# Low parts of later weights in the second scan instead of the first, three small operations on ScalarE, and transposes at the front of a unit

## The chip, the core and the metric

One Trainium2 chip, one of its cores. A core has TensorE (PE, matmuls and transposes; PEld is its weight load), VectorE (DVE), ScalarE (ACT), GpSimd (POOL) and SyncE (SP, which issues DMAs); DMAs are also issued on POOL's queue. Each engine works through its own instructions in the order in which they were written into the program. The metric is the device time of one execution in microseconds (us), the median of three.

## The reference

A hybrid layer for 512 tokens and 16 learned meta tokens, width 1024, all fp32. Two token mixers run on the same normalised input, and a channel mixer of experts follows them. What the change touches is the second token mixer (SSD, like Mamba-2), and the preparation of two weights of the expert part:

```python
xbc = jax.nn.silu(causal_dwconv(xbc, conv_w, conv_b))     # 4 taps
xs, Bm, Cm = split_cols(xbc, (SSD_D_INNER, SSD_BC, SSD_BC))

def ssd_chunk_step(S, inp):                               # chunks of 64 tokens
    xdt, a, Bc, Cc = inp
    acum = jnp.cumsum(a, axis=1)
    seg = jnp.exp(-jnp.abs(acum[:, :, None] - acum[:, None, :]))
    cb = jnp.einsum('btgn,bsgn->btsg', Cc, Bc)
    y = jnp.einsum('btsgr,btsg,bsgrp->btgrp', seg, cb, xdt)
    y = y + jnp.einsum('btgn,bgrpn,btgr->btgrp', Cc, S, jnp.exp(acum))
    to_end = jnp.exp(acum[:, -1:] - acum)
    S = S * jnp.exp(acum[:, -1])[..., None, None] + jnp.einsum('bsgn,bsgr,bsgrp->bgrpn', Bc, to_end, xdt)
    return S, y

y = y.reshape(Bsz, L, SSD_D_INNER) * jax.nn.silu(z)
y = rmsnorm(y.reshape(Bsz, L, SSD_GROUPS, SSD_D_INNER // SSD_GROUPS), ...)
```

The first mixer (GLA) is a chunked scan of the same kind with gates. In the expert part the weight w_q (here wpq, 16 blocks) and the table of down projections for a dense share of the experts (puT, 16 blocks) are multiplied with the normalised tokens.

## The kernel before, in words

Matmuls keep fp32 accuracy with three products of split operands: each operand is a high part (hi, rounded by ACT to the fast matmul type) and a low part (lo = raw − hi, by DVE). `unit` loads a weight block of 128x1024 on SP's queue (`raw`, three buffers), makes `whi` on ACT and `wlo` on DVE. For the 32 blocks of wpq and puT, which come late in the program, `unit_c` reads the low part back from DRAM (`lo_d`). Somebody has to make it earlier: that is `lows`, a generator with 64 steps, one for each half block of 128x512. A step loads `zr`, ACT copies it to `zh`, DVE subtracts in place (`zh<-zr,zh`) and a DMA on POOL's queue writes `lo_d<-zh`. The loads are on POOL's queue too (L148). `zh` has 2 buffers and `zr` 3, so ACT can begin a `zh` only when the `lo_d` write two steps before has landed. What is written is read first in the expert part, at about 814 us, some 120 us behind the last stage that the change touches.

The program ahead of the expert part has these stages. From about 80 to 302 us runs the first scan (`gproj`, `gscan`: projections q, k, v and the gate g, with tiles `vt`, `go`, `kn`, `ed`, and the chunk loop), with all 64 steps of `lows` merged into it. From 302 to 345 us come the rest of `sproj(0)` and the second scan's first decays. From 345 to 690 us the second scan runs: `sscan(g)` for four groups g of 8 heads, four chunk pairs of 128 tokens each, and beside it `sproj(g + 1)`, or, beside group 3, the gates of the merge.

`sproj(g)` has six convolution units (BT, CT, and four of xT) and then the projection z. A unit `conv` is 48 matmuls of 128x264 into `pa` and `pb`, two copies `rw` on ACT, the first tap on DVE (L287, which also adds the bias), three more taps on DVE (L289), and a silu (tanh on ACT, `silu_t`, and a DVE operation at L279). `turn(b)` transposes the xT of two units earlier (XLAG = 2) on PE into `px` (L310) and `pxm` (L313), and ACT copies them to `xs` and `xsm`.

`sscan(g)` does for each chunk pair: `ssp` (state contributions, L358), the DVE addition into `sS`, `py` (L425, 16 small matmuls with `xs`), `pi` (L429, L430, with the state `sS`), DVE operations on `y`, a square with sum on ACT, `ry` on DVE and POOL, the normalisation (L392, DVE), the transpose `pyt`, and, for the next chunk pair, `decays`: `pr` (L383, L384), a subtraction on DVE, the absolute value (L387, DVE: it masks the sign bit) and the exponential on ACT. `px`, `pxm`, `ssp`, `py`, `pi`, `pyt` and `pr` all take their PSUM tile from one ring of 4 buffers.

`drive((n, generator), ...)` merges generators by shares: each gets its turn in proportion to its n. Out of the order so written a scheduler sets each engine's instruction order, and the pools' buffer counts add waits.

## Time and profile before

| | us |
|---|---|
| three runs | 2184.10, 2188.85, 2195.99 |
| median | 2188.85 |
| the profiled execution | 2189.25 |
| its span | 2187.5 |
| PE busy in the span | 2083.8 (95%) |
| DVE busy | 1584.0 (72%) |
| ACT busy | 884.0 (40%) |
| POOL busy | 607.6 (28%) |

A span is cut into stages by their first matmuls; for each stage a view of the profile gives the busy time of each engine, the granted clock of PE and the share of the DMA engines. Another lists, for one engine and a stretch, what it waited for: the instruction that waited, the engine and instruction that released it, the sum, the count and the longest. A third lists single instructions in order of time with the idle time before each, and a fourth groups instructions by line and shape, with the mean duration of one.

### The profile page before, as it was taken

What the parts mean: (1) busy time and instruction counts of PE and PEld (TensorE: products, weight loads), DVE (VectorE), ACT (ScalarE), POOL (GpSimd) and SP (SyncE); (2) the same over time, 40 slices, a digit from 0 to 9 for tenths busy, and PEclk for the clock granted to TensorE, in tenths of its full rate; (3) what the DMA queues carried; (4) which work ended last, traced back from release to release, by engine and by line L of the source; (5) the groups of instructions that cost most, each with busy time, mean ns of one, the idle gap of its engine ahead of it and who ended that gap; (6) DMA issues with size and microseconds to landing.
All of it is one profiled execution on the core that took longest, in us unless ns stands there. A gap on an engine that the chain in (4) does not pass through costs nothing. (4 is left out here: it accounts for less than half of the span.)

```text
span 2187.5 us, 33055 instructions
## 1 busy us (share of the span) xinstructions
PE 2083.8 (95%) x12458; PEld 1825.2 (83%) x12458; DVE 1584.0 (72%) x2751; ACT 884.0 (40%) x1414; POOL 607.6 (28%) x564
## 2 busy tenths in 40 slices
PE   7988899999999998999999898999999999999997
PEld 6766778777777988989999887898998998898996
DVE  5374667787854668889899678877677777777775
ACT  5544433333333454455455432333333333333332
POOL 0253423343540000000000133343443333343331
PEclk9999999999999999999999999999999999999999
DMA  4557532212235877778667899989888888888883
GB/s 155 176 198 237 202 102 71 75 64 83 68 106 178 265 249 244 238 265 304 221 225 270 314 315 321 335 279 320 290 304 280 293 304 300 305 282 312 289 290 144
DMA packets 198432, 507.17 MB, mean 232 GB/s; under 512 B 16720, under 2 KB 89040, under 8 KB 196608
## 3 DMA queue, kind: packets, MB, share of 16 engines
q1 hardware_dynamic: 149440, 312.10, 42.2%
q0 software_dynamic: 48832, 192.96, 24.9%
q8 instruction: 97, 1.59, 0.3%
q14 instruction: 63, 0.52, 0.1%
HBM read 448.38 MB, written 56.62 MB: 231 GB/s over the span
## 5 line engine op out<-in xcount | busy, mean ns | idle before, releaser
L80 ACT ACTIVATE whi<-raw 128x1024 fp32r<-128x1024 f32 x433 | 458.5, 1059 | 517.4 <-PE pA L87 275.0
L83 DVE TENSOR_TENSOR wlo<-raw,whi 128x1024 fp32r<-128x1024 f32 x385 | 481.7, 1253 | 139.4 <-ACT whi L80 135.7
L86 PE MATMUL pA<-hh,whi 128*128 128x384 f32 x1024 | 346.3, 338 | 0.2 <-ACT ga L913 0.2
L88 PE MATMUL pA<-hh,wlo 128*128 128x384 f32 x1024 | 345.7, 338 | 0.5 <-DMA wlo<-lo_d 0.5
L87 PE MATMUL pA<-hl,whi 128*128 128x384 f32 x1024 | 345.9, 338 | 0.0
L989 POOL DMA_INDIRECT u<-in_pu,ix x128 | 176.4, 1378 | 298.9 <-ACT gh L1037 207.6
L989 POOL DMA_INDIRECT u<-in_pv,ix x128 | 170.9, 1335 | 281.0 <-ACT gh L1037 236.8
L1003 DVE SCALAR_TENSOR_TENSOR hacc<-u,acg,hacc 128x1024 f32<-128x1024 f32 x128 | 164.5, 1285 | 115.3 <-DMA u<-in_pv,ix 114.6
L1050 PE MATMUL va<-wlo,gh 128*128 128x512 f32 x768 | 239.9, 394 | 7.9 <-DVE wlo L83 7.9
L1050 PE MATMUL va<-whi,gh 128*128 128x512 f32 x768 | 239.7, 394 | 4.9 <-ACT whi L80 4.9
L997 DVE SCALAR_TENSOR_TENSOR scr<-u,hg 128x1024 f32<-128x1024 f32 x128 | 156.5, 1223 | 99.6 <-DMA u<-in_pu,ix 99.3
L87 PEld LDWEIGHTS pA<-hl,whi 128*128 128x128 f32 x1024 | 192.6, 188 | 4.2
L86 PEld LDWEIGHTS pA<-hh,whi 128*128 128x128 f32 x1024 | 192.1, 188 | 4.0 <-ACT ga L913 0.3
L1037 ACT ACTIVATE gh<-ga 128x384 fp32r<-128x384 f32 x128 | 67.2, 526 | 314.6 <-PE va L1050 293.7
L88 PEld LDWEIGHTS pA<-hh,wlo 128*128 128x128 f32 x1024 | 192.1, 188 | 0.7 <-DMA wlo<-lo_d 0.7
L1050 PEld LDWEIGHTS va<-wlo,gh 128*128 128x128 f32 x768 | 145.6, 190 | 40.6 <-DVE wlo L83 9.8
L1050 PEld LDWEIGHTS va<-whi,gh 128*128 128x128 f32 x768 | 144.4, 190 | 28.4 <-ACT whi L80 5.3
L86 PE MATMUL pk<-whi,hh 128*128 128x512 f32 x256 | 104.3, 407 | 6.7 <-ACT vt L80 6.3
L88 PE MATMUL pya<-oyh,wlo 128*128 128x256 f32 x384 | 108.5, 282 | 1.6 <-DVE wlo L83 1.6
L86 PE MATMUL pya<-oyh,whi 128*128 128x256 f32 x384 | 107.3, 280 | 0.0
L87 PE MATMUL pya<-oyl,whi 128*128 128x256 f32 x384 | 107.2, 279 | 0.0
L88 PE MATMUL pk<-whi,hl 128*128 128x512 f32 x256 | 102.3, 399 | 0.0
(910 smaller groups left out, 4473.9 us busy)
## 6 DMA issues: line engine op xcount, KB each, us to landing
raw<-in_puT SPq DMA_DIRECT2D x128, 512.0 KB
raw<-in_pv SPq DMA_DIRECT2D x128, 512.0 KB
raw<-in_wup SPq DMA_DIRECT2D x48, 512.0 KB
wlo<-lo_d SPq DMA_DIRECT2D x48, 512.0 KB
W_d<-stg POOLq DMA_DIRECT2D x12, 2048.0 KB
wb<-W_d SPq DMA_DIRECT2D x32, 768.0 KB
lo_d<-zh POOLq DMA_DIRECT2D x64, 256.0 KB
raw<-in_wpq SPq DMA_DIRECT2D x32, 512.0 KB
```

The source lines that it names most:

```text
L80: S.activation(out=o, in_=i, func=f, **kw)
L83: eng.tensor_tensor(o, x, y, op=op)
L86: T.matmul(o, lh, rh, start=first, stop=False)
L87: T.matmul(o, lh, rl, start=False, stop=False)
L88: T.matmul(o, ll, rh, start=False, stop=last)
L989: g_ = G.indirect_dma_start(out=u, out_offset=None, in_=a[tab], in_offset=bass.IndirectOffsetOnAxis(ap=ix[:, i, k:k + 1], axis=0))
L997: V.scalar_tensor_tensor(scr, u, 1.0, hg[:, i], op0=OP.mult, op1=OP.mult, accum_out=ac_[:, k:k + 1])
L1003: V.scalar_tensor_tensor(hacc[:, i], u, ac_[:, k:k + 1], hacc[:, i], op0=OP.mult, op1=OP.add)
L1037: i = S.activation(out=gh, in_=ga, func=AF.Copy)
L1050: T.matmul(va[t][c], x[:, cs], y[:, 512 * c:512 * c + 512], start=st_, stop=en_)
```

## The change

Four edits. The 64 steps of `lows` leave the first scan: they are merged with the end of `sproj(0)` (4 by the table), with the groups of the second scan (16 each) and the gates; `zh` gets 3 buffers and `zr` 4, in the pool `sg` of the second scan, and `zr` is loaded on SP's queue. The writes to `lo_d` stay on POOL's queue. The first tap, the absolute value and the normalisation become ACT activations (Identity with scale and bias, Abs, Copy with scale). And in a step of `sproj`, `turn` stands ahead of `conv` (or z) instead of behind it. The matmuls are the same in number and shape.

```diff
                 if 0 < n <= len(srcs):
-                    his[n - 1] = pool.tile([128, 512], F32R, name="zh", bufs=2)
+                    his[n - 1] = pool.tile([128, 512], F32R, name="zh", bufs=3)
                     act(his[n - 1], raws[n - 1], AF.Copy)
                 if n < len(srcs):
-                    raws[n] = pool.tile([128, 512], F32, name="zr", bufs=3)
-                    G.dma_start(raws[n], srcs[n])
+                    raws[n] = pool.tile([128, 512], F32, name="zr", bufs=4)
+                    nc.sync.dma_start(raws[n], srcs[n])
                 yield
...
                 cv = sp.tile([128, L], F32, name="cv")
-                V.tensor_scalar(cv, rw[:, 0:L], convw[:, b, 0:1], convb[:, b:b + 1], op0=OP.mult, op1=OP.add)
+                act(cv, rw[:, 0:L], AF.Identity, scale=convw[:, b, 0:1], bias=convb[:, b:b + 1])
...
                 for b in range(4 + XLAG):
+                    if b >= XLAG:
+                        turn(b - XLAG, x_[b - XLAG])
                     if b < 4:
                         x_.append(sp.tile([128, L], F32, name="xT", bufs=XLAG + 1))
                         conv(4 * g + b, x_[b])
                     else:
                         next(z_)
-                    if b >= XLAG:
-                        turn(b - XLAG, x_[b - XLAG])
                     yield
...
-                    V.tensor_scalar(sgm.bitcast(I32), sgm.bitcast(I32), 0x7FFFFFFF, None, op0=OP.bitwise_and)
+                    act(sgm, sgm, AF.Abs)
                     act(sgm, sgm, AF.Exp, scale=-1.0)
...
                 def norm(y, ry):
-                    V.tensor_scalar(y, y, ry, None, op0=OP.mult)
+                    act(y, y, AF.Copy, scale=ry)
...
-                lz = mix2.enter_context(tc.tile_pool(name="lz", bufs=1))
-                lw = lows(lz)
                 g1 = gproj(1)
-                drive((8, gscan(0)), (4, take(g1, 4)), (14, take(lw, 14)))
-                drive((8, g1), (32, take(lw, 32)))
+                drive((8, gscan(0)), (4, take(g1, 4)))
+                drive((8, g1))
                 p0 = sproj(0)
-                drive((8, gscan(1)), (6, take(p0, 6)), (20, lw))
+                drive((8, gscan(1)), (6, take(p0, 6)))
...
-            drive((4, p0))
+            lw = lows(sg)
+            drive((4, p0), (4, take(lw, 4)))
             for g in range(3):
-                drive((9, sscan(g)), (10, sproj(g + 1)))
-            drive((9, sscan(3)), (16 - NGT, gates(0, 16 - NGT, sg, 2)))
+                drive((9, sscan(g)), (10, sproj(g + 1)), (16, take(lw, 16)))
+            drive((9, sscan(3)), (16 - NGT, gates(0, 16 - NGT, sg, 2)), (16, lw))
```

What the scheduler makes of it is seen in the built order of each engine. The writes to `lo_d` show where the 64 steps come to stand: 16 ahead of group 0 (between the scans), 31 in group 0, 17 in group 1, none in groups 2 and 3.

On ACT, in the first scan, at the second projection of v (`vt` copies it out of PSUM; − is before, + after; the numbers behind pk count PSUM tiles):

```order
-L80 ACTIVATE zh<-zr 128x512 x2
-L80 ACTIVATE vt<-pk_1413 128x512
-L80 ACTIVATE vt<-pk_1414 128x512
-L80 ACTIVATE vt<-pk_1415 128x512
-L80 ACTIVATE zh<-zr 128x512
-L80 ACTIVATE vt<-pk_1416 128x512
+L80 ACTIVATE whi<-raw 128x1024 x3
+L80 ACTIVATE vt<-pk_1314 128x512
+L80 ACTIVATE vt<-pk_1315 128x512
+L80 ACTIVATE vt<-pk_1316 128x512
+L80 ACTIVATE vt<-pk_1317 128x512
 L80 ACTIVATE vm<-pke 16x512
```

The copies `zh` are gone from between the copies `vt`; only weights' high parts and `vt` are left.

On DVE, in group 0 of the second scan, the second half of a chunk pair, before (from the silu of one xT unit to that of the next):

```order
L279 SCALAR_TENSOR_TENSOR xT<-silu_t,cv 128x528
L83 TENSOR_TENSOR y<-y,xd 128x512
L387 TENSOR_SCALAR sgm<-sgm 128x512
L83 TENSOR_TENSOR y<-y,zt 128x512
L283 MEMSET rw 128x3
L83 TENSOR_TENSOR sgm<-sgm,cb 128x512
L83 TENSOR_TENSOR wlo<-raw,whi 128x1024
L176 TENSOR_SCALAR ry<-sy 128x1
L287 TENSOR_SCALAR cv<-rw,c_cst_96 128x528
L392 TENSOR_SCALAR y<-y,ry 128x512
L289 SCALAR_TENSOR_TENSOR cv<-rw,c_cst_96,cv 128x528 x3
L283 MEMSET rw 128x3
```

and the same place after:

```order
L83 TENSOR_TENSOR zh<-zr,zh 128x512
L83 TENSOR_TENSOR y<-y,zt 128x512
L83 TENSOR_TENSOR sgm<-sgm,cb 128x512
L83 TENSOR_TENSOR wlo<-raw,whi 128x1024
L176 TENSOR_SCALAR ry<-sy 128x1
L83 TENSOR_TENSOR zh<-zr,zh 128x512 x2
L289 SCALAR_TENSOR_TENSOR cv<-rw,c_cst_96,cv 128x528 x2
L83 TENSOR_TENSOR zh<-zr,zh 128x512
L289 SCALAR_TENSOR_TENSOR cv<-rw,c_cst_96,cv 128x528
L83 TENSOR_TENSOR zh<-zr,zh 128x512
L283 MEMSET rw 128x3
L279 SCALAR_TENSOR_TENSOR xT<-silu_t,cv 128x528
```

The tap of L287, the mask of L387 and the norm of L392 are gone, and five subtractions of lows stand in the stretch, two of them where the norm stood behind `ry`. At the start of a chunk pair `sS<-sS,ssp` now stands ahead of `wlo`, where it stood behind it.

On PE, in group 0, around the transposes `px`, `pxm` (L310, L313) and the chunk pair's `ssp` and `py`, before:

```order
L253 MATMUL pa<-hh,wlo 128x264
L253 MATMUL pb<-hh,wlo 128x264
L310 MATMUL px<-c_cst_79,xT 128x128 x4
L313 MATMUL pxm<-c_cst_79,xT 16x128
L358 MATMUL ssp<-xw,bt 128x512 x2
L425 MATMUL py<-xs,sgm 64x64 x16
L429 MATMUL pi<-sS,CT 64x512
```

and the same transposes after:

```order
L253 MATMUL pa<-hh,wlo 128x264
L253 MATMUL pb<-hh,wlo 128x264
L310 MATMUL px<-c_cst_79,xT 128x128 x4
L313 MATMUL pxm<-c_cst_79,xT 16x128
L250 MATMUL pa<-hh,whi 128x264
L251 MATMUL pa<-hl,whi 128x264
L250 MATMUL pb<-hh,whi 128x264
```

Behind the transposes comes now a whole convolution unit of 48 matmuls, and only then `ssp` and `py`, where before these two followed at once.

## Rows read from the trace of the kernel before

**Rows 1.** The page, part 1: busy us, share of the span, instructions.

```profile
PE 2083.8 (95%) x12458; PEld 1825.2 (83%) x12458; DVE 1584.0 (72%) x2751; ACT 884.0 (40%) x1414; POOL 607.6 (28%) x564
```

**Rows 2.** Stages: stretch, length, busy us (count) by engine, PE clock, DMA share, GB/s.

```profile
80.00:302.00 222.00, 194.39 (x1035) 155.13 (x1034) 131.81 (x186) 96.33 (x183) 96.06 (x147) 0.94 0.63 209
302.00:345.00 43.00, 42.22 (x240) 34.52 (x240) 23.73 (x36) 14.39 (x33) 11.70 (x10) 1.00 0.23 77
345.00:434.00 89.00, 82.90 (x614) 67.34 (x612) 70.53 (x95) 31.35 (x61) 36.00 (x31) 0.98 0.21 69
```

**Rows 3.** Waits of PE, 80 to 302: total us, times, longest us.

```profile
PE pkd L635 <- DVE ed L83: 8.7, 4, 4.0
PE pk L86 <- ACT vt L80: 6.3, 4, 3.7
PE pa L250 <- DVE go L279: 4.3, 1, 4.3
...
PE pb L250 <- DVE go L279: 2.3, 1, 2.3
```

**Rows 4.** Waits of ACT, 80 to 302, same columns.

```profile
ACT zh L80 <- DMA lo_d<-zh: 62.9, 37, 3.8
ACT zh L80 <- DMA zr<-in_puT: 12.2, 5, 4.7
```

**Rows 5.** Timeline of ACT: start, us, instruction [idle before <- releaser].

```profile
211.63 0.63 ACT L80 ACTIVATE zh<-zr 128x512 fp32r<-128x512 f32 x1 [1.98 <-DMA lo_d<-zh]
212.16 1.55 ACT L80 ACTIVATE vt<-pk 128x512 f32<-128x512 f32 x3
```

**Rows 6.** Two short stretches, columns as in rows 2.

```profile
130.00:133.00 3.00, 2.27 (x11) 2.27 (x12) 2.35 (x2) 0.60 (x1) 3.00 (x5) 0.50 0.00 0
213.00:217.00 4.00, 4.00 (x9) 2.61 (x9) 0.17 (x1) 1.54 (x4) 1.08 (x2) 0.50 0.97 357
```

**Rows 7.** Waits of PE, 302 to 690.

```profile
PE py L425 <- ACT xsm L80: 12.6, 6, 2.9
PE pi L430 <- DVE sS L83: 4.0, 3, 1.3
```

**Rows 8.** Timeline of all engines in group 0's second chunk pair.

```profile
385.69 0.64 ACT L80 ACTIVATE silu_t<-cv 128x528 f32<-128x528 f32 x1 [5.32 <-DVE cv L289]
...
388.47 1.21 PE L425 MATMUL py<-xs,sgm 64*64 64x64 f32 x32 [2.83 <-ACT xsm L80]
...
391.67 0.68 DVE L83 TENSOR_TENSOR sS<-sS,ssp 128x512 f32<-128x512 f32 x1
```

**Rows 9.** Convolution half of group 0's stretch, and a part of it; columns as rows 2.

```profile
355.00:412.60 57.60, 52.07 (x410) 43.05 (x411) 51.07 (x71) 19.17 (x38) 25.89 (x23) 0.97 0.20 68
373.00:385.00 12.00, 12.00 (x98) 11.60 (x98) 11.14 (x17) 3.40 (x7) 6.82 (x6) 1.00 0.13 45
```

**Rows 10.** Timeline of PE: pr, which ends one chunk pair and opens the next.

```profile
371.60 0.50 PE L383 MATMUL pr<-R,bdr 128*128 128x512 f32 x1
...
392.32 0.72 PE L383 MATMUL pr<-R,bdr 128*128 128x512 f32 x1
```

**Rows 11.** Groups, 80 to 302: xcount | busy us, mean ns | idle before <- releasers.

```profile
L83 DVE TENSOR_TENSOR zh<-zr,zh 128x512 fp32r<-128x512 f32 x64 | 47.3, 745 | 62.6 <-ACT zh L80 62.5
...
L80 ACT ACTIVATE zh<-zr 128x512 fp32r<-128x512 f32 x64 | 40.1, 632 | 85.6 <-DMA lo_d<-zh 62.9 <-DMA zr<-in_puT 12.2 <-DMA zr<-in_wpq 5.7
...
L142 POOL DMA_DIRECT2D lo_d<-zh x64 | 35.4, 554 | 105.1 <-DVE zh L83 100.9 <-DVE qe L83 3.2 <-DVE tdt L83 0.9
```

**Rows 12.** Groups of DVE, 300 to 610, same columns.

```profile
L287 DVE TENSOR_SCALAR cv<-rw,c_cst 128x528 f32<-128x528 f32 x20 | 13.8, 689 | 0.0
L387 DVE TENSOR_SCALAR sgm<-sgm 128x512 int32<-128x512 int32 x12 | 12.7, 1056 | 0.0
...
L392 DVE TENSOR_SCALAR y<-y,ry 128x512 f32<-128x512 f32 x12 | 8.2, 680 | 14.0 <-POOL ry L83 14.0
```

**Rows 13.** Group of ACT, 300 to 610: the exponential.

```profile
L80 ACT ACTIVATE sgm<-sgm 128x512 f32<-128x512 f32 x12 | 7.6, 633 | 29.6 <-DVE sgm L387 28.0 <-DVE rw L283 1.6
```

## The prediction

> **What bounds the kernel now.** The page comes first: TensorE (PE) is busy 95% of the span [rows 1], so a gain can come only from the gaps between its matmuls, or from time in which its clock is low. The table of stages then says where these are. PE loses 222 − 194.4 = 27.6 us to gaps in the first scan, at a mean clock of 0.94; between the scans 0.8 us; and in each group of the second scan 89 − 82.9 = 6.1 us at 0.98 [rows 2] (groups 1 and 2, in the next two stretches, read alike within 0.5 us). The change touches nothing behind these stretches, so about 27.6 + 13.3 (222 x 0.06 of clock) + 3 x 7.9 = 65 us is all that it could win.
>
> The waits of PE in the first scan name four that come to 21.6 us: pkd for DVE's ed, pk for ACT's vt, pa and pb for DVE's go [rows 3]. What stands in front of vt is seen on ACT: it waited 62.9 us for the landing of lo_d<-zh, and 12.2 us for the load zr [rows 4]. ACT works in order; its zh at 211.63 waited 1.98 us for such a landing, and vt came right behind it at 212.16 [rows 5]. A gap also costs clock: the granted clock was 0.50, the 1.2 GHz level, for 3 us at 130 and for 4 us at 213, behind gaps of 4.0 and 3.7 us [rows 3, 6].
>
> In the second scan PE waits for the copy xsm ahead of py (12.6 us in 6 times) and for sS ahead of pi (4.0 in 3) [rows 7]: two py waits and one pi wait a group, 5.5 us. In the one at 388.47 (2.83 us), px and pxm hold the PSUM buffer that py wants, and their copies stood on ACT behind silu_t, which had waited 5.32 us for DVE's cv [rows 8]. But DVE is as near to being the bound: in the four units of convolution from 355 to 412.6 us it is busy 51.1 of 57.6 us [rows 9], and the pr at 392.32 ends a chunk of 20.7 us (371.60 to 392.32) [rows 10] right behind DVE's second sS, at 391.67 [rows 8].
>
> **The change part by part.** The sum is made against the profiled 2189.25 us, 0.4 above the median of the three runs.
>
> *First scan without lows.* The 64 lows take from ACT 64 x 0.632 = 40.1 us, from DVE 64 x 0.745 = 47.3 us and from POOL 64 x 0.554 for lo_d (and as much for the loads) [rows 11]. Their work lies beside PE; on the path are the waits behind them. I count all of vt but 0.1 (6.2), both go (6.6), 3.5 of the 8.7 of ed (the wait of 4.0 is cut to half, and one of 2.2 loses the DVE tap in front of it), 0.8 of small ones: 17.1 us. The other ed waits stay: no low stands ahead of the one of 2.0. Of the 13.3 us of clock the two stretches at 0.50 alone are 3.5; I take 8, since the gaps that go are the long ones. Together −25; bounds −15 (idle alone, a little of it replaced) and −29 (11.9 of clock).
>
> *Between the scans* 16 lows come to stand, some 13 of them ahead of z's first silu_t on ACT. With three zh buffers ACT is held by each for the landing, 62.9 / 37 = 1.7 us a wait [rows 4], 22 us for 13, and ACT has 43 − 14.4 = 28.6 free [rows 2]. So it nearly fits: +2. Bounds 0 and 16 x 0.45 = +7.2, where 0.45 is what a low cost in the first scan, (17.1 + 11.9) / 64.
>
> *Groups 0 and 1* take the other 48: by the order 31 and 17, none in groups 2 and 3. Per group ACT gets 6 taps, 4 abs and 4 norms, all near its 0.633 for the exponential of the same size: 8.9 us, and 31 x 0.632 = 19.6; 31.4 + 28.5 = 60 of 89 us. POOL goes to 36 + 17 = 53 of 89. Both have room. DVE in a group's convolution half loses 5 x 0.689 + 3 x 1.056 + 2 x 0.680 = 8.0 us [rows 12] and gets 16 or 17 lows at 0.8 (0.745, a little longer as POOL works beside it), 13.6: 51.1 − 8.0 + 13.6 = 56.7 us of work for 57.6 of time. If DVE keeps its present 6.5 us of idle time, a half takes +5.6; if it has none, −0.9. The norms take with them their wait for POOL's ry, 14.0 / 12 = 1.2 us each [rows 12], 2.3 of the 6.5 in a half: with the other 4.2 kept, 56.7 + 4.2 = 60.9, +3 for group 0, and I take +2 for group 1 with its 16: +5 in all. That wait for ry is now ACT's, and rw, xs, xsm and silu_t are queued behind it, for which PE and DVE wait; 1.2 us is under the 5.9 that px gains (below), so it adds nothing; without that lead it would cost up to 2 x 1.2 a half, within the 5.6. The taps come behind their own rw, and an abs stands where ACT waited for the same tile already: they add no wait. The rest of group 0, the z half, has 31.4 us, for DVE now 70.5 − 51.1 = 19.4; with 15 lows and less 3.1 it has 28: this hides.
>
> *Group 2 (beside group 3's projection), without lows, with all three moves.* px and pxm stand one whole convolution unit (48 matmuls; 98 of them take 12.0 us in a stretch that holds little else [rows 9], so 5.9) ahead of ssp and py, so their copies are done when py comes: the py wait of chunk 1 goes, 12.6 / 3 − 2.83 = −1.4; pi's goes, 4.0 / 3 = −1.3, since sS now stands ahead of wlo on DVE. The wait of 2.83 in chunk 2 goes too, but the chunk is then paced by DVE, which loses two taps and an abs there: 2.4 us. Sum −5; bounds −7 (with the 1.8 of clock) and 0. Group 3 runs beside the gates and had no px: 0.
>
> *Loads of zr on SP.* A load that waits for its zr buffer now has the weight loads (raw) behind it on SP's queue. They run up to three units ahead and none of the waits [rows 3, 4, 7] is for raw, so nothing; if that cover went, one late unit per group would cost about what the late zr did once in the first scan, 4.3 (its zh, then silu_t, go and pa) [rows 3, 4], which the range holds.
>
> A rule speaks against the moves to ACT: the Trainium skill, "ScalarE: Activation LUTs", section "Rules for kernel authors", wants multiplications and additions on VectorE, up to about three times faster for each element in bf16. Here the data are fp32, and DVE is no faster in this trace, 0.69, 1.06 and 0.68 against 0.63 us [rows 12, 13]. By the rule DVE would be relieved of a third, an estimate of 2.1 us instead of 8.0 in a half, and the sum would be about 2180.
>
> **Sum:** −25 + 2 + 5 − 5 = −23: 2189.25 − 23 = 2166 us; own range 2155 to 2176.
>
> **Rivals.** *More: DVE isn't the bound.* Against 56.7 of 57.6 speaks that DVE's idle time comes of waits for ACT, and these fall. Then groups 0 and 1 win as group 2 does, with its clock: −25 + 2 − 5.4 x 3 = −39, **2150**.
>
> *The first scan's gaps are its own.* A chain kn, ed, vt, go may find PE as early without lows; then only the two longest are won, vt's 3.7 and go's 4.3 [rows 3]: −8 + 2 + 5 − 5 = −6, **2183**. Against it: vt right behind a held zh [rows 5].
>
> *The lows' landings hold ACT in the second scan.* Each of the 48 waits 1.7 us, 82 us on ACT, and rw, xs and silu_t stand behind. In the first scan 80.8 us of such waits (62.9 and the loads) gave 17.1 to 20 of gaps on PE, a quarter: +20, so −23 + 20 = −3, **2186**. For it: DVE is 89% busy there; against it: a third buffer, loads from SP, and few bytes beside (DMA 0.21 against 0.63 [rows 2]). The Trainium skill, "SBUF — State Buffer", section "SBUF: two separate sides", says that DMAs issued on the POOL queue can starve for descriptors while DVE holds the port pair that the two share; by that, lo_d would land late here, with this rival's time. In this trace the issue of lo_d took 0.554 us beside a DVE busy 59%, which shows no such hold.
>
> *Slower: DVE stands idle behind each low.* DVE is in order as well, and a low's subtraction waits for its zh. In the first scan DVE stood 62.6 us before 64 of them, 0.98 each [rows 11]. There it had 90 us to spare, here it has 6.5 a half. At 0.745 + 0.98 = 1.73 a low, the halves are 51.1 − 8.0 + 27.7 (29.4 for 17) = 70.8 and 72.5 against 57.6, +13 and +15, and the z half of group 0 19.4 − 3.1 + 26 = 42 against 31.4, +11: +39, in place of +5. −25 + 2 + 39 − 5 = +11, **2200**. It decides from 0.95 us of idle time per low on; at 0.75 it is no change. Against it: in the order up to six lows stand in places where DVE waits anyway (behind ry, ahead of y's norm).
>
> **Chances.** Forecast 0.48; more 0.17; own gaps 0.09; landings 0.15; idle DVE 0.11. The likeliest is 2166. About 0.5% (2178 to 2200) is what a measurement here can tell from no change. Faster by more: 0.46 of the forecast, all of "more", 0.03 of "own gaps", 0.66. Slower by more: 0.07 of "idle DVE" and 0.03 of "landings" at twice the price, 0.10. The same: the rest, 0.24. The range leaves out the upper end: 2146 (the best bounds of the scan and of the groups) to 2189.
>
> **What would show it.** In the profile after, the first scan is some 25 us shorter, PE waits there are under 6 us for vt and go together, and its clock is 0.97 or more. No py waits for xsm. In groups 0 and 1 DVE is over 90% busy, and they stay within 5 us of 89; group 2 takes 84. I am wrong if the first scan's PE waits turn up unchanged with other names, if ACT's zh waits over 1.5 us for lo_d with PE waiting for rw or xs behind it, or if a new wait for raw appears.

## The result and the profile after

The changed kernel takes 2199.55 us (median of five, 2197.16 to 2206.2), the kernel before 2188.35 in the same comparison: 1.006 times as long, interval 1.0033 to 1.0088. The profiled execution has a span of 2200.3 us, against 2187.5. The forecast was 2166; the time lies where the rival "slower" put it, but, as the runs show, not for its reason.

The page's first part, and the table of stages cut at the same times as [rows 2] (the fourth and fifth row are the stretches behind it):

```profile
PE 2096.3 (95%) x12458; PEld 1829.5 (83%) x12458; DVE 1549.7 (70%) x2695; ACT 924.2 (42%) x1470; POOL 587.5 (27%) x500
```

```profile
80.00:302.00 222.00, 210.67 (x1187) 168.84 (x1187) 95.31 (x141) 73.42 (x149) 31.27 (x26) 0.98 0.20 67
302.00:345.00 43.00, 33.02 (x177) 27.98 (x175) 27.95 (x33) 21.23 (x36) 17.46 (x23) 0.88 0.81 272
345.00:434.00 89.00, 79.14 (x519) 60.92 (x518) 74.64 (x99) 47.26 (x87) 54.50 (x55) 0.92 0.61 203
434.00:523.00 89.00, 77.49 (x533) 61.83 (x534) 73.05 (x95) 49.78 (x92) 51.73 (x52) 0.92 0.56 186
523.00:611.00 88.00, 84.35 (x620) 67.69 (x619) 59.06 (x78) 41.09 (x74) 36.99 (x31) 1.00 0.22 72
```

PE has 12.5 us more of busy time for the same 12458 matmuls, and more of them ran at the lower clock: from 302 to 523 the table has 0.88 to 0.92. The stretch 80 to 302 is now nearly full (210.7 of 222, before 194.4) and its clock 0.98. But 302 to 345 has fallen from 42.2 to 33.0, with the DMA engines busy 0.81, and the two groups behind it from 82.9 and 82.5 to 79.1 and 77.5. The stretch from 523 on is better than before.

Since the work shifts against fixed times, I follow two kinds of marks on PE: the last transpose pot of the first scan, and each pr that opens a chunk pair. Their rows (duration min/median/max, first and last start), from the views of line L599's tile and of line L383, before and after:

```profile
L599 PE MATMUL pot<-c_cst,osb x32: 270/273/329, 145.7 to 318.8; 128*128 128x128 f32 x32
L599 PE MATMUL pot<-c_cst,osb x32: 271/273/329, 136.6 to 295.6; 128*128 128x128 f32 x32
```

```profile
L383 PE MATMUL pr<-R,bdr x16: 473/499/776, 354.9 to 666.0; 128*128 128x512 f32 x16
L383 PE MATMUL pr<-R,bdr x16: 473/499/796, 345.3 to 677.7; 128*128 128x512 f32 x16
```

Read off the timelines in the same way (us):

| | last pot | to first pr | group 0 | group 1 | group 2 | group 3 (3 pairs) | last pr |
|---|---|---|---|---|---|---|---|
| before | 318.8 | 36.1 | 88.6 | 88.7 | 87.5 | 46.3 | 666.0 |
| after | 295.6 | 49.8 | 101.4 | 100.1 | 84.6 | 46.3 | 677.7 |
| difference | −23.2 | +13.7 | +12.8 | +11.4 | −3.0 | 0 | +11.7 |

The last column is nearly the whole effect: behind the last pr both kernels do the same, in 1521.5 and 1522.6 us. Over all kernels below, that tail took 1514.2 to 1522.6 us, though nothing in it differs except the lo_d reads of some; why it varies stays open. So stages are compared here rather than spans. The mark pot isn't exact either: in the changed kernel and the nine below that keep its first scan, with the same instructions and no low, it lies between 290.7 and 295.6. So the first scan's prices, each from one trace, hold to some 5 us. The groups repeat better: with the moves and no low in it, group 0 or 1 takes 85.8 to 86.2 us in every kernel.

In the first scan the waits for vt and go [rows 3] are gone, as forecast; the one for ed has stayed, 8.3 us after 8.7, where 3.5 were to go:

```profile
PE pkd L635 <- DVE ed L83: 8.3, 4, 2.2
PE po L659 <- DVE gS L574: 1.4, 5, 0.3
```

In the second scan the wait for xsm [rows 7] is gone too, but the one for sS has grown from 4.0 us to 16.1, and there are new ones, for zt and at px:

```profile
PE pi L430 <- DVE sS L83: 16.1, 7, 3.7
PE pa L250 <- DVE zt L279: 9.4, 3, 7.1
PE px L310 <- DVE rw L283: 2.9, 1, 2.9
```

One of them, in group 0's second chunk pair, which took 25.0 us instead of 20.7, in the timeline of all engines:

```profile
373.67 2.92 DVE L83 TENSOR_TENSOR zh<-zr,zh 128x512 fp32r<-128x512 f32 x2
...
376.00 1.01 POOL L83 TENSOR_TENSOR ry<-ry,mhalf 128x1 f32<-128x1 f32 x1
...
376.98 1.14 POOL L142 DMA_DIRECT2D lo_d<-zh  x2
377.05 0.72 ACT L80 ACTIVATE y<-y,ry 128x512 f32<-128x512 f32 x1 [2.53 <-POOL ry L83]
...
380.70 0.63 ACT L80 ACTIVATE zh<-zr 128x512 fp32r<-128x512 f32 x1 [2.26 <-DVE cv L289]
...
381.36 0.69 DVE L83 TENSOR_TENSOR zh<-zr,zh 128x512 fp32r<-128x512 f32 x1 [1.51 <-ACT zh L80]
...
382.60 0.68 DVE L83 TENSOR_TENSOR sS<-sS,ssp 128x512 f32<-128x512 f32 x1
...
383.33 1.11 PE L430 MATMUL pi<-sS,CT 128*64 128x512 f32 x1 [3.16 <-DVE sS L83]
```

ACT waits 2.53 us for POOL's ry, in front of its norm (the norm was on DVE before). Then its zh at 380.70 comes 2.26 us late. The profile names a cv of DVE as the last to end, which this copy doesn't read, and the load of this zr had been issued at 371.40, 9 us before. What fits is the buffer. zh has three, so this one takes over from the low three before it. That low is the first of the two subtractions of 373.67, done at 375.1; its write could go only at 376.98, since POOL was at its own sgm, xd and ry, in order. 3.7 us later ACT begins, and a write in these kernels lands some 4 us after its issue (the list of DMA issues of e13, below). DVE's next subtraction waits 1.51 us for that zh, sS stands behind it, and PE's pi waits 3.16 us for sS. It is one chain through POOL, ACT and DVE, each in order; that the buffer is what ACT waited for is read from the times, the trace doesn't name it. What the waits come to in the stretch 302 to 545:

```profile
ACT zh L80 <- DMA lo_d<-zh: 25.8, 24, 2.6
ACT y L80 <- POOL ry L83: 19.6, 7, 4.8
```

```profile
POOL lo_d L142 <- DVE zh L83: 62.0, 39, 4.2
POOL R L83 <- PE pr L384: 15.5, 7, 4.7
```

```profile
L83 DVE TENSOR_TENSOR zh<-zr,zh 128x512 fp32r<-128x512 f32 x64 | 54.3, 856 | 22.8 <-ACT zh L80 22.5
```

POOL stands 62.0 us at writes that wait for a subtraction, with R, sS and ry behind them in its queue. Of what POOL makes, other engines wait only for ry (ACT, the 19.6 us above) and for sS (DVE, 1.3 us).

### The profile page after: what moved, and what is told of

The parts are those of the page before. It is cut to its first block, busy times and chain, and to the rows that moved or that the text cites. A ratio compares the mean times of both kernels' runs of the same rounds, so it can differ in the third digit from the quotient of the medians.

```text
span 2200.3 us, 32999 instructions
## 1 busy us (share of the span) xinstructions
PE 2096.3 (95%) x12458; PEld 1829.5 (83%) x12458; DVE 1549.7 (70%) x2695; ACT 924.2 (42%) x1470; POOL 587.5 (27%) x500
## 5 line engine op out<-in xcount | busy, mean ns | idle before, releaser
L988 POOL DMA_INDIRECT u<-in_pv,ix x128 | 175.7, 1373 | 277.9 <-ACT gh L1036 233.6
L1036 ACT ACTIVATE gh<-ga 128x384 fp32r<-128x384 f32 x128 | 67.2, 525 | 319.6 <-PE va L1049 294.8
```

Source lines behind the costliest of these rows:

```text
L988: g_ = G.indirect_dma_start(out=u, out_offset=None, in_=a[tab], in_offset=bass.IndirectOffsetOnAxis(ap=ix[:, i, k:k + 1], axis=0))
L1036: i = S.activation(out=gh, in_=ga, func=AF.Copy)
```

## The experiments

Where an edit has several lines, the lines that matter stand here. "Moves" are the three operations on ACT; "the price of the lows" is what a kernel takes longer in a stretch than the same kernel without lows.

### What the lows cost in either place: e1, e2

```diff
-            nc.sync.dma_start(lo.bitcast(F32), lo_d[n])
+            nc.sync.dma_start(lo.bitcast(F32), lo_d[0])
-                    [a["wpq"][b] for b in range(NQ)] + [a["puT"][b] for b in range(NL)] for c in range(2)]
+                    [a["wpq"][0]] for c in range(2)]
```

> The kernel before with 2 of the 64 lows only (the others are left out, and every later read takes block 0, so these low parts are wrong). It measures what the lows cost in the first scan. In the profile of the changed kernel the first scan ends 23 us earlier than before. If that came of the lows alone (theory A), this kernel takes 2188 - 23 = 2165 us and its second scan is as before, 88.6 us a group. If the other edits had a part in it (the convolution units at the scan's end have their first tap on ACT), it gains under 18.

> The changed kernel with 2 of the 64 lows only, the same parts left out. Theory A: the stretch between the scans, group 0 and group 1 are 14, 13 and 11 us longer than before because of the lows there; without them the stretch is as before and the groups take 85 us, as group 2 does. Then this kernel takes 2200 - 14 - 16 - 14 = 2156 us. Rival B: the three operations that went to ACT make it late for PE (ACT's norm waits 19.6 us for POOL's ry in groups 0 and 1), and the lows only add a little: the groups stay over 95 us, and it takes 2176 us or more.

e1 took 2160.74 us (ratio 0.986, 0.9839 to 0.988), e2 2158.9 (0.9847, 0.9828 to 0.9867). By the marks: e1 has its last pot at 296.5 and everything behind it to 0.1 as before (36.1, 88.6, 88.6, 87.5); e2 has 294.8, then 39.9, 85.9, 85.9, 84.6. So the lows' price is 318.8 − 296.5 = 22.3 us in the first scan. In the changed kernel it is 49.8 − 39.9 = 9.9 between the scans, 15.5 in group 0 and 14.2 in group 1: 39.6. By these marks theory A holds and B falls: without lows a group with the moves is 2.7 us shorter, not longer.

What the price of the groups consists of is seen when they are cut at their own marks: groups 0 and 1 of the changed kernel, then group 0 of e2 (its group 1 reads alike; columns as rows 2):

```profile
345.30:446.70 101.40, 90.08 (x610) 70.67 (x609) 84.38 (x111) 57.16 (x104) 58.84 (x62) 0.93 0.65 217
446.70:546.80 100.10, 89.33 (x610) 69.99 (x609) 74.65 (x98) 49.51 (x91) 49.99 (x48) 0.93 0.45 150
334.90:420.80 85.90, 82.21 (x610) 65.92 (x610) 59.12 (x81) 40.98 (x75) 37.04 (x31) 1.00 0.23 74
```

PE runs the same 610 matmuls. Of the 29.7 us in the two groups 14.7 are more gaps between them, and 15.0 are more busy time: the clock is 0.93 in place of 1.00, which alone would make 82.2 us into 88.4 (an estimate, 82.2 / 0.93).

### The moves and the transposes, with the lows left in the first scan: e3, e9

```diff
 # e9: the three moves alone; e3 has also
+                    if b >= XLAG:
+                        turn(b - XLAG, x_[b - XLAG])
                     if b < 4:
...
-                    if b >= XLAG:
-                        turn(b - XLAG, x_[b - XLAG])
```

> The kernel before with the moves to ACT and the transposes first in a unit, and the lows left where they were, in the first scan. Theory A: groups 0 to 2 take 85 us each in place of 88.6, the rest is as before: 2188 - 10 = 2178 us. Rival B: the groups are longer than 88.6 and it takes 2195 us or more.

> The kernel before with the three operations on ACT alone; transposes and lows as before. With the transposes first as well, a group takes 85.9 us in place of 88.6 (chunk pairs 14.3, 18.3, 19.6, 33.7 in place of 16.7, 20.7, 18.6, 32.5), and the stretch between the scans 3.6 us more. If DVE paces the second chunk pair, as the forecast said, the moves alone bring it to 18.5 us, and the first keeps its wait for xsm, 16.7. If the place of the transposes is what counts, both stay at 16.7 and 20.7. The 3.6 us should then be there with the moves alone, or not at all.

e3: 2185.35 us, ratio 0.9972 (0.9957 to 0.9987), with the groups as theory A has them but not its 2178 us; e9: one run, 2181.18 beside 2190.58 of before. Groups 0 to 2:

| | to first pr | chunk pairs of group 0 | groups 0, 1, 2 |
|---|---|---|---|
| before | 36.1 | 16.7, 20.7, 18.6, 32.5 | 88.6, 88.7, 87.5 |
| e9, moves | 37.2 | 14.3, 19.2, 18.9, 33.5 | 85.9, 85.9, 84.6 |
| e3, moves and transposes | 39.7 | 14.3, 18.3, 19.6, 33.7 | 85.9, 85.9, 84.6 |

The moves alone give the 8.4 us of the groups, and the first pair its 2.4 us, which I had expected to stay. The transposes first in a unit shift the boundary between pairs 2, 3 and 4 and win nothing in sum; between the scans they cost 2.5 us. There PE comes to px before DVE has made its xT (the 2.9 us of px in the waits above; e2 has the same wait with no low near it).

### Which part of a low costs: e4, e5, e6

```diff
 # e4
-                    tt(V, h, r, h.bitcast(F32), OP.subtract)
+                    pass
 # e5
-                    act(his[n - 1], raws[n - 1], AF.Copy)
-                    tt(V, h, r, h.bitcast(F32), OP.subtract)
+                    tt(V, h, r, r, OP.subtract)
 # e6, and reads of block 0
-                    G.dma_start(lo_d[b, :, 512 * c:512 * c + 512], h.bitcast(F32))
+                    if b == 0:
+                        G.dma_start(lo_d[b, :, 512 * c:512 * c + 512], h.bitcast(F32))
```

> The changed kernel without the lows' subtractions on DVE (what is written back is the high part). Against the changed kernel without lows, the lows cost 9.9 us between the scans, 15.5 in group 0 and 14.2 in group 1, 39.6 in all. Theory A1, DVE: their 64 x 0.86 us of work and the waits for zh stand on DVE in front of the scan's own steps, and without them at least 25 of the 39.6 come back, span 2175 us or less. Rival A2, ACT held by the landings of lo_d: the waits stay, under 12 come back, span 2188 us or more.

> The changed kernel without the lows' copies on ACT (DVE writes zr - zr into zh, so the low parts are zero): DVE waits for a load only, never for ACT, and ACT for no landing. Theory A1 in the form of DVE's work alone: what DVE has to do is as before, and under 15 of the 39.6 us come back, span 2185 us or more. If it is the waits that the chain through ACT brings (ACT held by the landing, DVE held by ACT), at least 25 come back, span 2175 us or less.

> The changed kernel with the write of only the first block of lo_d (the other writes are left out, every later read takes block 0): no landing holds a zh buffer, and 62 of 64 writes are missing on POOL's queue. Theory A2: at least 25 of the 39.6 us come back, span 2175 us or less, in every part. Theory A1: DVE's work and its place stay; the 10 us between the scans may come back, for there the DMA engines are busy 0.81, but the groups keep 13 us or more each, span 2188 us or more.

Each of the three ran once. From the last pot to the last pr the changed kernel takes 382.1 us, without lows 342.7. e4 takes 384.0, e5 396.5, e6 363.1: prices of 41.3, 53.8 and 20.4 in place of 39.4. Taking DVE's part away wins nothing, taking ACT's costs 14 us more; taking the writes away wins half. A1 in its plain form, DVE, falls, and so does the idea that the hop over ACT is to blame. A2 is right for 19 us, not for 25. In these kernels the lows also come to stand elsewhere: in group 1 the changed kernel has 16 copies zh, e4 has none and e6 four, so an edit changes the crowd ahead of group 1 as well, and the prices are of the whole arrangement.

### Work against transfers: e14, e15

```diff
 # e14: zr loaded four times, then read again; only block 0 is written, and all reads take it
-                    raws[n] = pool.tile([128, 512], F32, name="zr", bufs=4)
-                    nc.sync.dma_start(raws[n], srcs[n])
+                    raws[n] = zrs[n % 4]
+                    if n < 4:
+                        nc.sync.dma_start(raws[n], srcs[n])
 # e15: no copy, no subtraction
-                    G.dma_start(lo_d[b, :, 512 * c:512 * c + 512], h.bitcast(F32))
+                    G.dma_start(lo_d[b, :, 512 * c:512 * c + 512], r)
```

> The changed kernel with the lows' work on ACT and DVE and without their transfers: zr is loaded four times only and read again for every low, and only the first block of lo_d is written (all later reads take it). No low waits for a transfer. Theory E, the waits: what a low costs beside the second scan is the time in which ACT and DVE, in order, stand at a zh whose load or buffer hasn't landed, with sS and silu_t behind it; without transfers the 39.6 us (over the changed kernel without lows, from the last pot to the last pr) fall to 10 or less. Rival A1, the work: 64 x (0.63 on ACT + 0.86 on DVE) stays, and with it 20 us or more.

> The changed kernel with the lows' transfers and without their work: zr is loaded on SP and written to lo_d from there on POOL's queue; no copy on ACT, no subtraction on DVE. What is left is the share of the DMA engines and the queues of SP and POOL. Theory E and rival A1 both expect little, under 8 of the 39.6 us, since no instruction of ACT or DVE waits. Rival F, the queues and the transfers themselves (raw behind zr on SP; R and ry behind lo_d on POOL; late landings of raw): 15 us or more stay.

One run each, and in both no low is left in group 1. e14: 359.0 us between the marks, a price of 16.4. e15: 386.5, a price of 43.9, though no instruction of ACT or DVE is left of the lows. Theory E's lower price came only in part, and its expectation for e15 was wrong: it is F that holds. Waits of PE and POOL in e15:

```profile
PE py L425 <- POOL sgm L83: 14.9, 1, 14.9
```

```profile
POOL lo_d L142 <- DMA zr<-in_wpq: 38.7, 18, 4.7
POOL lo_d L142 <- DMA zr<-in_puT: 30.5, 20, 3.4
```

POOL stands 69 us at writes that wait for their load, and the scan's product sgm, which py needs, waits behind them on POOL: one gap of 14.9 us. DVE waits 29.7 us there for POOL's sS, 1.3 in the changed kernel, so e15 shows something that the changed kernel has much less of. A DMA issued on POOL's queue isn't free work beside the engine's own: with an unmet wait it holds POOL's tensor operations.

### The queues: e8, e7

```diff
 # e8
-                    nc.sync.dma_start(raws[n], srcs[n])
+                    G.dma_start(raws[n], srcs[n])
 # e7
-                    G.dma_start(lo_d[b, :, 512 * c:512 * c + 512], h.bitcast(F32))
+                    nc.sync.dma_start(lo_d[b, :, 512 * c:512 * c + 512], h.bitcast(F32))
```

> The changed kernel with the loads zr back on POOL's queue. Rival C: the loads zr wait on SP for their buffers with the weight loads raw behind them (SP waited 95 us for zh in 51 of them), and the late raw is what makes the stretch between the scans and the groups long: then most of 38 us come back, 2175 us or less. Theory A: raw is not what PE waits for, and POOL has its own work (ry, R) behind waiting loads: 2195 to 2210 us.

> The changed kernel with the writes of lo_d on SP's queue, so that POOL's ry and R stand behind no low. ACT's norm waits 19.6 us for ry in groups 0 and 1. If POOL's queue is what makes ry late and ACT late, 8 us or more of the 39.6 come back, span 2192 us or less, and the wait for ry falls below 12 us. If ry is late because of DVE and POOL's own tensor operations, the wait stays, and SP, which now waits for subtractions with the weight loads behind it, makes it no better: span 2197 us or more.

e8: 2206.5 us, ratio 1.0076 (1.0053 to 1.0099), a price of 46.5 between the marks, 7 more than with the loads on SP. By the medians the two kernels can't be told apart (1.0076 and 1.006). e7: one run, 2178.27 beside 2188.06; by the marks 370.4, a price of 27.7, so 12 us come back (7 between the scans, 4 in group 1); the rest of the run's lead lies before the last pot and in the tail. ACT's waits there:

```profile
ACT y L80 <- POOL ry L83: 23.5, 8, 6.2
ACT zh L80 <- DMA zr<-in_wpq: 15.4, 11, 4.9
...
ACT zh L80 <- DMA lo_d<-zh: 10.0, 8, 3.1
```

The wait for a write fell from 25.8 to 10.0 us. The wait for ry didn't fall (23.5 against 19.6), so ry isn't what POOL's queue makes late, and the reason that I gave in the expectation was wrong while its number was right.

### Where the lows stand: e13, e12, e11

```diff
 # e13: 16 for each group, first loads held back by one element of the group's z; no transposes first
+                    if n % 16 < 4:
+                        V.tensor_copy(raws[n][0:1, 0:1], P_[n // 16][4][0:1, 3, 0:1])
 # e12: moves; 40 lows in the first scan, 24 held back to group 3
+            lw = lows(sg, 40, 64, 3, 4, nc.sync, lambda: P_[3][4][0:1, 3, 0:1])
+            drive((9, sscan(3)), (16 - NGT, gates(0, 16 - NGT, sg, 2)), (26, lw))
 # e11: moves; lows in the first scan with
-                    his[n - 1] = pool.tile([128, 512], F32R, name="zh", bufs=2)
+                    his[n - 1] = pool.tile([128, 512], F32R, name="zh", bufs=3)
-                    raws[n] = pool.tile([128, 512], F32, name="zr", bufs=3)
+                    raws[n] = pool.tile([128, 512], F32, name="zr", bufs=2)
```

> The changed kernel with the transposes back behind the convolution and the lows held to 16 for each of the four groups (one element of the group's z is copied into the first four zr of each 16). Between the scans there are none. Theory D, the crowd: 64 lows in the 140 us behind the first scan stand in front of z and of sS and wait for their landings; at 16 a group they cost a third or less, under 13 us in all: 2188 - 22 - 8 + 13 = 2171 us or less. If a low has its price of 0.5 us or more wherever it stands beside the second scan, 30 us or more: 2188 us or more.

> The three moves to ACT; 40 lows in the first scan as before, the other 24 in group 3 of the second scan and behind it (a copy of one element of group 3's z holds their first loads back). There is no convolution beside group 3: DVE is busy 42 of 79 us and ACT 27. If the price of a low follows what room DVE has (theory A1'), 24 cost nearly nothing in group 3, and the first scan gains 22.3 x 24 / 64 = 8 us: 2173 us. If a low costs the same anywhere, 0.35 us at least, nothing is won: 2181 us.

> The kernel before with the three moves to ACT, the lows in the first scan, and there zh with 3 buffers and zr with 2 instead of 2 and 3. The moves alone gave 2181 us; the first scan loses 22.3 us to the lows. In the trace of before ACT's zh waits there 62.9 us for landings of lo_d and 18 us for loads. If the landing is what sets that price, a third zh buffer wins 8 us or more of it, 2173 us or less; if it is each low's own place on ACT and DVE, the price stays within 3 us, 2178 to 2184.

e13: 2194.35 us, ratio 1.0027 (1.0011 to 1.0044). The groups take 98.0, 95.9, 96.3 and, to the last pr, 57.2; against e9's 339.9 us between the marks it has 384.6, a price of 44.7 or 0.70 a low. Spreading them over the groups doesn't help (held back, the 16 of a group crowd in its first two chunk pairs: 20.7 and 25.2 us instead of 14.3 and 19.2). Theory D falls. The list of DMA issues of its stretch 296 to 520 (count, KB each, median us from issue to landing) has the landing of a write that was used above:

```profile
zr<-in_wpq SPq DMA_DIRECT2D x32, 256.0 KB, 4.0
lo_d<-zh POOLq DMA_DIRECT2D x32, 256.0 KB, 4.2
```

e12: 2180.46 (0.9965, 0.9944 to 0.9986): 24 lows less in the first scan bring pot to 308.1, 9.3 us earlier than e9's, and the three pairs of group 3 take 12.8 us more. Even beside the gates, with DVE half idle, a low costs about 0.5 us. e11: 2181.76 (0.9968, 0.995 to 0.9986), pot at 320.2: a third zh for a zr wins nothing, ACT now waits for loads instead.

### The queues in the first scan: e16, e19, e17, e18

```diff
 # e16: moves, write on SP; e19: moves, load on SP; e17: moves, both on SP; e18: both on SP and no other edit
-                    G.dma_start(lo_d[b, :, 512 * c:512 * c + 512], h.bitcast(F32))
+                    nc.sync.dma_start(lo_d[b, :, 512 * c:512 * c + 512], h.bitcast(F32))
...
-                    G.dma_start(raws[n], srcs[n])
+                    nc.sync.dma_start(raws[n], srcs[n])
```

> The three moves to ACT, the lows in the first scan as before, their writes on SP's queue in place of POOL's. With the moves alone the first scan's last pot is at 317.4 us, 22 later than without lows. In the second scan the same change of queue won 12 us between the first scan's end and the last pr. If the write's way through POOL is what makes a low dear, the first scan wins 6 us or more, pot at 311 or earlier; if the chain of two zh buffers is as slow by SP, it stays within 3 us of 317.

> The three moves to ACT, the lows in the first scan, their loads zr on SP's queue (as the change has them) and their writes on POOL's. Last pot: both on POOL 317.4, write on SP 311.0, both on SP 301.3. If it is the waiting write on POOL that hurts (POOL's work behind it), this stays at 312 or later, about 2178 us. If loads and writes count alike, 307 to 311, 2172 us.

> As the kernel with the writes on SP in the first scan, and the loads zr on SP as well, so that POOL issues nothing for the lows. If POOL's own operations there (go, ke, qn, ro) are late behind the lows' DMAs, this is faster than with the writes alone by 3 us or more; if the weight loads behind zr and lo_d on SP are late, it is slower, and PE waits for units of q, k, v.

> The kernel before with one edit: the lows' loads and writes are issued on SP's queue instead of POOL's. With the three moves to ACT as well, the last pot of the first scan came at 301.3 us in place of 317.4. Theory F, POOL's queue: in the kernel before, POOL stood 100.9 us at writes waiting for zh, with its own go, ke and ro behind; without the moves the scan is as short, pot at 300 to 304, the groups stay at 88.6 us, 2188 - 16 = 2172 us. If the moves had a part in it (the convolution taps on ACT), pot comes at 309 or later, 2179 us.

| | write | load | last pot | median, ratio (interval) |
|---|---|---|---|---|
| e9, moves | POOL | POOL | 317.4 | 2181.18 (one run) |
| e19 | POOL | SP | 324.4 | 2186.1, 0.9984 (0.9969 to 0.9999) |
| e16 | SP | POOL | 311.0 | 2169.75, 0.9917 (0.9891 to 0.9942) |
| e17 | SP | SP | 301.3 | 2160.9, 0.9877 (0.9849 to 0.9905) |
| e18, no moves | SP | SP | 298.9 | 2164.78, 0.9862 (0.9836 to 0.9887) |

e18 is the kernel before with two words changed. Its waits of PE and POOL in the first scan, beside [rows 3]:

```profile
PE pkd L635 <- DVE ed L83: 7.0, 4, 2.2
PE pa L250 <- DVE go L279: 3.1, 2, 2.7
PE pk L86 <- ACT vt L80: 2.0, 2, 1.5
...
PE pkm L587 <- DVE km L83: 1.0, 1, 1.0
```

```profile
POOL go L83 <- DVE go L279: 157.4, 6, 91.7
POOL ro L83 <- DVE ro L176: 64.6, 7, 14.3
```

The waits for vt and go are down from 6.3 and 6.6 to 2.0 and 3.6, with all 64 lows in place, and POOL waits for its own inputs, not at writes. What POOL's queue did before can be seen in the kernel before, in the timeline around the zh that waited 4.7 us for its load [rows 4]:

```profile
230.73 0.69 DVE L83 TENSOR_TENSOR zh<-zr,zh 128x512 fp32r<-128x512 f32 x1 [0.62 <-ACT zh L80]
...
235.33 0.55 POOL L142 DMA_DIRECT2D lo_d<-zh  x1 [3.06 <-DVE zh L83]
...
235.88 1.08 POOL L148 DMA_DIRECT2D zr<-in_puT  x2
...
241.10 0.63 ACT L80 ACTIVATE zh<-zr 128x512 fp32r<-128x512 f32 x1 [4.68 <-DMA zr<-in_puT]
...
243.11 0.59 PE L250 MATMUL pa<-hh,whi 128*128 128x264 f32 x1 [4.30 <-DVE go L279]
...
243.85 1.29 POOL L83 TENSOR_TENSOR go<-go,gnw 128x512 f32<-128x512 f32 x1
```

The subtraction that frees the buffer of the load at 235.88 is that of 230.73, which ended at 231.4; but the load stands on POOL behind a write that waits 3.06 us for a later subtraction. It is issued 4.5 us late, ACT's zh waits 4.68 us for it, DVE's subtraction and go stand behind, and PE waits 4.30 us for go: that is the longest wait for go of [rows 3]. POOL's own go, at 243.85, had its input at 243.05 and lost 0.8 us. In the whole scan ro is the only product of POOL that another engine waits for (DVE, 4.0 us in the kernel before, 5.5 in e18). So what the standing queue made dear here isn't POOL's own work, the reason that I gave in the expectation of e18, but the lows themselves, with vt and go in order behind them. With both transfers on SP, ACT stands 78.3 us ahead of its copies zh instead of 85.6 [rows 11], and less of it for a write's landing, 62.9 us before [rows 4], and in e18:

```profile
ACT zh L80 <- DMA lo_d<-zh: 42.2, 25, 4.6
```

With the load moved alone (e19) POOL stands longer at writes (188.2 us), again with only ro waited for, 4.2 us; what is worse is ACT. It stands 102.8 us before its copies zh, against 90.8 in e9, 81.6 in e16 and 75.2 in e17, the same order as their last pots. PE's wait for vt in e19, after 6.3 us in [rows 3]:

```profile
PE pk L86 <- ACT vt L80: 13.7, 3, 9.5
```

The price of the lows in the first scan falls from 22.3 us to 298.9 − 296.5 = 2.4 (e18 against e1), which is within the 5 us of the mark. Of the 24.5 us between the two profiled spans 19.9 lie before the last pot and 5.1 in the tail; the groups take 0.5 back. Why SP's queue makes the lows so much cheaper, the runs don't separate. The loads stand behind waiting writes there too: in sum they are issued 80 us after their buffer is free in e18, 101 us in the kernel before, and 2 us in e19, the slowest of the moves' kernels. The writes are issued in sum 4 us after their subtraction in e18 and 26 us in the kernel before. And from SP a write lands sooner, 3.1 us after its issue (e18; the last number, a median) against 3.9 from POOL's queue (e19):

```profile
lo_d<-zh POOLq DMA_DIRECT2D x64, 256.0 KB, 3.9
lo_d<-zh SPq DMA_DIRECT2D x64, 256.0 KB, 3.1
```

e17 and e18 beat both kernels: 2160.9 and 2164.78 us against 2188 and 2199.55. By the marks, e17's last pr is at 641.2, e18's at 646.6.

## Why the prediction was wrong, step by step

- **What bounds the kernel, and what could be won:** right. PE sets the end, and the gain of 65 us at most was counted in the right stages.
- **First scan, −25 (−15 to −29):** right, −23.2; e1 gives −22.3 for the lows alone. The waits for vt and go went; the 3.5 us of ed that the sum has did not (8.7 to 8.3). The rival that the gaps are the scan's own falls.
- **Between the scans, +2 (0 to +7.2): wrong, +13.7.** Two things were mis-sized. The lows cost 9.9 there, above the upper bound: I summed ACT's free time, as if silu_t could use what a waiting zh leaves. How long ACT would stand before a zh was about right (17.7 us in the stretch, 22 forecast), but one such place cost PE 7.1 us, waiting for zt. And the transposes first in a unit, which I had costed at nothing there, add 2.5 us, and the moves 1.1 (e9, e3).
- **Groups 0 and 1, +5: wrong, +24.2.** This is the step that failed most. With the moves' gain counted, the lows cost 29.7 us there. I made DVE's work the measure (56.7 of 57.6 us), but e4, without any of it, is no faster. In its place the runs show two things. Half of the price, 15.0 us, is PE's own work at a lower clock, a term that I had for the first scan and put at nothing here. The other half, 14.7, is gaps, from a chain of waits: a low goes through ACT, DVE and POOL, in order on each. Writes wait for subtractions and behind POOL's own work, a zh for a write's buffer, and sS behind a zh, for which PE waits 16.1 us (4.0 before). I had given POOL 53 of 89 us of work and so room; a busy time says nothing of a queue that stands. Which link costs how much stays open (below).
- **Group 2, −5: the direction right, the size off and the reason partly wrong, −3.0.** Pairs 1 and 2 won 2.4 and 2.5 us, about the 5 expected, pairs 3 and 4 gave 0.9 and 1.0 back. And the new place of px isn't needed for it: in e9, without it, the wait for xsm falls from 12.6 us to 2.8, with 4.4 for xs beside it, and the groups take the same 84.6 to 85.9.
- **Loads on SP, nothing:** the choice of queue was no loss (e8, with them on POOL, takes 7 us more by the marks), but the first scan shows that it helps only if the write leaves POOL too (e19, e17).
- **The rule on ScalarE:** the Trainium skill's page "ScalarE: Activation LUTs", section "Rules for kernel authors", would have kept the tap and the norm, multiplications and additions, on DVE. e9 shows the three moves together winning 8.4 us in the groups. The measurement decides; it fits DVE's 51.1 of 57.6 us [rows 9].
- **The rival "slower", 2200:** the time is its time, the mechanism is not. Its condition was 0.95 us of DVE idle time for each low; the row above has 22.8 / 64 = 0.36, and e4, where no low is on DVE, costs the same. **"Landings", 2186,** was nearer in kind: the writes make 12 (e7) to 19 us (e6) of the price. But ACT waited 25.8 us for landings, not 82, and of such a wait I took a quarter and left out what stands behind it on DVE. The Trainium skill, "SBUF — State Buffer", section "SBUF: two separate sides", advises to issue such DMAs elsewhere than on POOL; the runs agree with that advice, e18 by 26 us. They show no stretched issue (0.558 us a write in the changed kernel, 0.554 before). They do show writes landing later, 3.9 us after their issue from POOL's queue and 3.1 from SP's in the first scan, though not why, and POOL in order behind unmet waits.

Left open: how the 39.6 us in the second scan divide by cause, and what it is about the queue that wins the first scan's 20. Work without transfers costs 16.4, transfers without work 43.9, so the parts don't add up; an edit moves the crowd as well.

## What to carry to other kernels

A side job is priced by the queues it waits in and by what stands behind it there, not by the engine time that it needs: before moving it elsewhere, look for the queue that stands at one of its waits, and try its DMAs, loads and writes together, on another. Here two words did that in place, for 26 us less, where moving the job next to a busier stage cost 17 us more than it had cost before. And when a change bundles several edits, price each: of the four here, the moves gained 8 us, the transposes lost 2.5, the new place lost 17, and without the new queue of the loads it would by the marks have lost some 7 more.

## What the runs showed of the hardware that I hadn't expected

- A DMA on POOL's queue with an unmet wait holds POOL's tensor operations: py waited 14.9 us for POOL's sgm in a kernel whose lows were transfers only (e15). POOL stood 100.9 us in the first scan of the kernel before; there that held back the lows' own loads (one by 4.5 us), and of POOL's products only ro was waited for, 4.0 us.
- The same 64 lows, on the same engines, cost 22.3 us with both transfers on POOL's queue and 2.4 with both on SP's (e1, e18; each price to some 5 us), and more than either with the load alone on SP (e19, pot 7.0 us later than e9's).
- Three fp32 operations on 128x528 and 128x512 tiles took no longer on ACT than on DVE when taken together, 2.18 against 2.43 us: the tap and the norm were longer on ACT, the abs shorter. In groups 2 and 3 of the changed kernel they took (abs and exponential are one group, sgm)

```profile
L80 ACT ACTIVATE sgm<-sgm 128x512 f32<-128x512 f32 x16 | 10.1, 631 | 8.6 <-DVE sgm L83 8.2 <-DVE rw L283 0.2
L80 ACT ACTIVATE y<-y,ry 128x512 f32<-128x512 f32 x8 | 5.8, 724 | 13.4 <-POOL ry L83 13.4
...
L80 ACT ACTIVATE cv<-rw,c_cst 128x528 f32<-128x528 f32 x6 | 5.0, 828 | 0.1
```

against 0.689, 1.056 and 0.680 us for tap, abs and norm on DVE [rows 12].
